# A pooling kernel: where the stores and the small first load are issued

## The chip, the cores and the metric

The kernel runs on one core of a Trainium2 chip. The metric is device time in microseconds, the median of several executions. One execution of each kernel was also recorded by the hardware profiler; its views are what is read here.

## What is computed

The input is 32 x 256 x 4096 values in fp32 (134.22 MB). The output takes every four neighbours along the last axis and gives the square root of the mean of their squares (p = 2), 32 x 256 x 1024 values (33.55 MB):

```python
for i in range(out_length):
    window = np.abs(x[:, :, 4*i:4*i+4]) ** p
    result[:, :, i] = (np.mean(window, axis=-1)) ** (1.0 / p)
```

Windows never cross a row, so the kernel treats the input as one flat array.

## The kernel before

The flat array is cut into 20 **loads**, L0 to L19, of 128 partitions x 13184 values each (6.75 MB; the last one is 10808 wide), and one **odd piece** of 840 x 128 values (0.43 MB), laid out as 30 partitions x 3584. Three input tiles (`xt`) take the loads in turn, so L3 goes into the tile of L0, and so on. Two output tiles (`ot`, 128 x 6592) take the results. Two loads make one **group** and share an output tile; the last two loads are groups of their own whose results go into a free input tile.

Each load goes through these steps:

- **SP** issues the DMA that brings the load (line 82). It waits until VectorE (DVE) has summed the load that held the tile before.
- **ScalarE (ACT)** squares the tile in place (line 168).
- **DVE** sums every four squares into the output tile: one reduce for the first 15 loads (line 111), two adds for the later ones (lines 122 and 124). One part of load 18 is squared on DVE (line 165).
- When a group is summed, **ACT** takes the roots in place (line 102, the function `root`). A group's root is put on ACT's queue one load later (two for group 8), behind the next load's square.
- A **store** (line 99, the function `store`) takes the group out. Groups 0 to 6 are stored from ACT's queue; groups 7 to 10 (`late`) from SP's queue, behind all loads.

The odd piece is loaded first (line 132) into part of an output tile, squared and summed on DVE (lines 137 and 139), rooted on ACT (line 143) and stored from ACT's queue (line 144). Its root and store stand at the head of ACT's queue, before L0's square.

The order on each engine is the order in which the program calls its instructions: the scheduling is manual, and each engine works through its queue in order. A DMA issue is an instruction of the queue that it is on: it waits there for its data, and what stands behind it waits too. Transfers of SP's queue and of ACT's queue run on the same DMA engines.

In the kernel before, `root` does not store: it puts the group into the list `held`, and the main loop empties the list after it has put the next square and its sum on their queues:

```python
            total_sum(ots[g][:, summed:summed + step // k], v, i)

            while held:
                store(held.pop(), nc.scalar)
            while pending and pending[0][0] <= done - LAGS.get(pending[0][1], 1):
                root(*pending.pop(0)[1:])
```

Of the kernel before, what the change touches and what calls it, by code (L numbers as in the profile page):

```python
# [9 lines left out]
def kernel(  # L10
# [15 lines left out]
    nc = tc.nc  # L26
# [5 lines left out]
    P = nc.NUM_PARTITIONS  # L32
    fp32 = mybir.dt.float32
    Act = mybir.ActivationFunctionType
    xf = x.rearrange("b c l -> (b c l)")
    of = out.rearrange("b c l -> (b c l)")
    total = xf.shape[0] // P
# [5 lines left out]
    ODD = 840  # L43
# [26 lines left out]
    def block(flat, g, div):  # L70
        at, width = sum(columns[:g]) * P // div, columns[g] * P // div
        return flat[at:at + width].rearrange("(p w) -> p w", p=P)
# [4 lines left out]
    def load(i):  # L77
        s, at, w, _ = loads[i]
        v = x_tiles[s % X_SLOTS][:, at:at + w]
        g = group_of[i]  # L80
        src = sum(loads[j][2] for j in range(firsts[g], i))
        nc.sync.dma_start(out=v, in_=block(xf, g, 1)[:, src:src + w])  # L82
        xs[i] = v
# [10 lines left out]
    def follows(ins, before):  # L94
        for b in before:
            tc.declare_no_dep(ins.ins, b.ins, reason="follows from other waits")

    def store(g, queue):
        stores[g] = queue.dma_start(out=block(of, g, k), in_=ots[g])

    def root(g, o, ends):
        r = nc.scalar.activation(out=o, in_=o, func=Act.Sqrt, scale=1.0 / k)  # L102
        follows(r, by_act[:-1] + list(stores.values()))
        by_act.append(r)
        if ends and g not in late:
            held.append(g)

    def total_sum(o, v, i):
        add = mybir.AluOpType.add
        if i < PAIRS:  # L110
            r = nc.vector.tensor_reduce(  # L111
                out=o, in_=v.rearrange("p (n j) -> p n j", j=k),
                axis=mybir.AxisListType.X, op=add,
            )
            follows(r, sums[:-1])
            sums.append(r)
            return

        q = v.rearrange("p (n j) -> p n j", j=k)
        front = v[:, 0:v.shape[1] // 2]  # L120
        h = front.rearrange("p (n j) -> p n j", j=2)
        r = nc.vector.tensor_tensor(out=h, in0=q[:, :, 0:2], in1=q[:, :, 2:4], op=add)  # L122
        follows(r, sums[:-1] + by_load)
        r = nc.vector.tensor_tensor(out=o, in0=h[:, :, 0], in1=h[:, :, 1], op=add)  # L124
        follows(r, sums[:-1])
        sums.append(r)


    Q = 30
    odd = ODD * P // Q  # L130
    t = o_tiles[1][0:Q, 0:odd]
    nc.sync.dma_start(out=t, in_=xf[(total - ODD) * P:total * P].rearrange("(p w) -> p w", p=Q))  # L132
    ahead = 0
    while ahead < n and loads[ahead][0] < X_SLOTS:
        load(ahead)
# [4 lines left out]
        out=o, in_=t.rearrange("p (n j) -> p n j", j=k),  # L140
# [4 lines left out]
        out=of[(total - ODD) * P // k:total * P // k].rearrange("(p w) -> p w", p=Q), in_=o,  # L145
    )
    pending = []
    held = []
    done = 0
    for i in range(n):  # L150
        s, _, w, chunks = loads[i]
        while ahead < n and loads[ahead][0] < s + X_SLOTS:
            load(ahead)
            ahead += 1
        g = group_of[i]
        if i == firsts[g]:
            t, first = (o_tiles[g % O_SLOTS], 0) if g not in in_x else (x_tiles[in_x[g][0]], in_x[g][1])
            ots[g] = t[:, first:first + columns[g] // k]
            summed = rooted = 0
        assert sum(chunks) == w  # L160
        c = 0
        for step in chunks:
            v = xs[i][:, c:c + step]
            if (i, c) in ON_DVE:
                r = nc.vector.tensor_tensor(out=v, in0=v, in1=v, op=mybir.AluOpType.mult)  # L165
                follows(r, sums[:-1])
            else:
                r = nc.scalar.activation(out=v, in_=v, func=Act.Square)  # L168
                follows(r, by_act[:-1])
                by_act.append(r)  # L170
            total_sum(ots[g][:, summed:summed + step // k], v, i)

            while held:
                store(held.pop(), nc.scalar)
            while pending and pending[0][0] <= done - LAGS.get(pending[0][1], 1):
                root(*pending.pop(0)[1:])
            done += 1
            c += step
            summed += step // k
            ends = summed == columns[g] // k  # L180
            if ends or i in FINE or (i in ENDS and c == w):
                pending.append((done - 1, g, ots[g][:, rooted:summed], ends))
                rooted = summed
    for job in pending:
        root(*job[1:])
# [37 lines left out]
```

## Time and profile before

| | |
|---|---|
| Median of 3 runs | 394.55 us (393.78 to 394.77) |
| Profiled execution | 393.78 us |
| Its span | 392.0 us |
| DVE busy | 274.5 us (70%) |
| ACT busy | 275.3 us (70%) |
| Moved by DMA | 167.77 MB, 428 GB/s over the span |
| A load on SP's queue, issue to landing | 31.6 us (median of 19) |
| A store on ACT's queue, issue to landing | 27.2 us (median of 7) |
| The odd load, the odd store | 3.9 us, 7.1 us |
| One square, one reduce, one root (full size) | 11.19 us, 13.89 us, 5.68 us |

The span is the time from the first to the last event of the profiled execution; its own time is 1.78 us longer. In the profile's rows, `L168` is line 168 of the kernel; `xt<-in_x_dram` is a load, `out_dram<-ot` a store; `SPq` and `ACTq` are DMA issues on SP's and ACT's queues. What stands in brackets at the end of a timeline row is the idle time of the engine before it, and what ended that. The windows view gives, for a stretch of time, the busy time and count of instructions on DVE, ACT and GpSimd, then a clock that does not matter here (no TensorE work), the DMA share (the packets' own time, counted at their end, as a share of 16 engines' time: over short stretches it jumps above 1) and the rate in GB/s.

### The profile page before, as it was taken

What the parts mean: (1) busy time and instruction counts of PE and PEld (TensorE: products, weight loads), DVE (VectorE), ACT (ScalarE), POOL (GpSimd) and SP (SyncE); (2) the same over time, 40 slices, a digit from 0 to 9 for tenths busy, and PEclk for the clock granted to TensorE, in tenths of its full rate; (3) what the DMA queues carried; (4) which work ended last, traced back from release to release, by engine and by line L of the source; (5) the groups of instructions that cost most, each with busy time, mean ns of one, the idle gap of its engine ahead of it and who ended that gap; (6) DMA issues with size and microseconds to landing.
All of it is one profiled execution on the core that took longest, in us unless ns stands there. A gap on an engine that the chain in (4) does not pass through costs nothing.

```text
span 392.0 us, 183 instructions
## 1 busy us (share of the span) xinstructions
DVE 274.5 (70%) x36; ACT 275.3 (70%) x38; POOL 0.2 (0%) x4
## 2 busy tenths in 40 slices
DVE  5207898885769476948693869386939690989991
ACT  1095879909890999099909990998099809987991
POOL 0000000000000000000000000000000000000000
DMA  9899999899999999999899999999989998999997
GB/s 367 379 444 452 452 447 441 347 444 468 447 401 431 471 431 393 431 474 431 387 431 474 431 457 441 393 431 468 436 387 431 474 431 387 447 452 401 446 439 330
DMA packets 4554, 167.77 MB, mean 428 GB/s; under 512 B 526, under 2 KB 526, under 8 KB 556
## 3 DMA queue, kind: packets, MB, share of 16 engines
q1 hardware_dynamic: 3501, 144.04, 85.3%
q10 hardware_dynamic: 1053, 23.73, 14.1%
HBM read 134.22 MB, written 33.55 MB: 428 GB/s over the span
## 4 chain that ended last, share of the span: by engine, by line
DMA 56%; DVE 22%; ACT 19%; SPq 0%; issue 0%
DMA xt<-in_x_dram 56%; ACT xt L168 19%; DVE ot L111 18%; DVE xt L122 3%; DVE ot L124 1%; DVE xt L124 1%; ACT xt L102 1%; SPq L132 0%; SPq L82 0%
## 5 line engine op out<-in xcount | busy, mean ns | idle before, releaser
L168 ACT ACTIVATE xt<-xt 128x13184 f32<-128x13184 f32 (+4 forms) x23 | 217.4, 9458 | 97.0 <-DMA xt<-in_x_dram 97.0
L111 DVE TENSOR_REDUCE ot<-xt 128x3296 f32<-128x13184 f32 x15 | 208.3, 13885 | 88.0 <-ACT xt L168 88.0
L102 ACT ACTIVATE ot<-ot 128x6592 f32<-128x6592 f32 x9 | 51.1, 5680 | 0.0
L122 DVE TENSOR_TENSOR xt<-xt 128x3296 f32<-128x3296 f32 (+5 forms) x9 | 34.5, 3835 | 16.5 <-ACT xt L168 16.4
L124 DVE TENSOR_TENSOR ot<-xt 128x3296 f32<-128x3296 f32 (+1 forms) x4 | 10.9, 2733 | 0.1
L143 ACT ACTIVATE ot<-ot 30x896 f32<-30x896 f32 x1 | 0.9, 948 | 10.5 <-DVE ot L139 10.5
L124 DVE TENSOR_TENSOR xt<-xt 128x1448 f32<-128x1448 f32 (+4 forms) x5 | 7.0, 1409 | 0.2
L137 DVE TENSOR_TENSOR ot<-ot 30x3584 f32<-30x3584 f32 x1 | 3.9, 3878 | 4.7 <-DMA ot<-in_x_dram 4.7
L102 ACT ACTIVATE xt<-xt 128x3296 f32<-128x3296 f32 (+3 forms) x4 | 5.8, 1445 | 1.1 <-DVE xt L124 1.1
L165 DVE TENSOR_TENSOR xt<-xt 128x5792 f32<-128x5792 f32 x1 | 6.2, 6182 | 0.0
L139 DVE TENSOR_REDUCE ot<-ot 30x896 f32<-30x3584 f32 x1 | 3.9, 3874 | 0.0
L143 ACT ACT_TABLE_LOAD x1 | 1.3, 1283 | 0.7 <-PEq L204 0.7
L204 POOL MEMSET const-bfloat16-1.0<- 128x1 bf16 x1 | 0.1, 103 | 0.0
L204 POOL MEMSET const-uint8-127<- 128x1 uint8 x1 | 0.1, 103 | 0.0
L204 POOL MEMSET const-float32-1.0<- 128x1 f32 x1 | 0.1, 100 | 0.0
L204 POOL MEMSET const-float32-0.0<- 128x1 f32 x1 | 0.1, 99 | 0.2 <-issue 0.2
## 6 DMA issues: line engine op xcount, KB each, us to landing
xt<-in_x_dram SPq DMA_DIRECT2D x19, 6592.0 KB, 31.6
out_dram<-ot ACTq DMA_DIRECT2D x7, 3296.0 KB, 27.2
out_dram<-ot SPq DMA_DIRECT2D x2, 3296.0 KB, 23.9
xt<-in_x_dram SPq DMA_DIRECT2D x1, 5404.0 KB, 23.9
out_dram<-xt SPq DMA_DIRECT2D x1, 1648.0 KB, 11.0
out_dram<-xt SPq DMA_DIRECT2D x1, 1351.0 KB, 6.6
ot<-in_x_dram SPq DMA_DIRECT2D x1, 420.0 KB, 3.9
out_dram<-ot ACTq DMA_DIRECT2D x1, 105.0 KB, 7.1
```

Of the source, the lines that this page charges most:

```text
L102: r = nc.scalar.activation(out=o, in_=o, func=Act.Sqrt, scale=1.0 / k)
L111: r = nc.vector.tensor_reduce(out=o, in_=v.rearrange("p (n j) -> p n j", j=k), axis=mybir.AxisListType.X, op=add,)
L122: r = nc.vector.tensor_tensor(out=h, in0=q[:, :, 0:2], in1=q[:, :, 2:4], op=add)
L124: r = nc.vector.tensor_tensor(out=o, in0=h[:, :, 0], in1=h[:, :, 1], op=add)
L137: nc.vector.tensor_tensor(out=t, in0=t, in1=t, op=mybir.AluOpType.mult)
L139: nc.vector.tensor_reduce(out=o, in_=t.rearrange("p (n j) -> p n j", j=k), axis=mybir.AxisListType.X, op=mybir.AluOpType.add,)
L143: nc.scalar.activation(out=o, in_=o, func=Act.Sqrt, scale=1.0 / k)
L165: r = nc.vector.tensor_tensor(out=v, in0=v, in1=v, op=mybir.AluOpType.mult)
L168: r = nc.scalar.activation(out=v, in_=v, func=Act.Square)
L204: nc = _bacc.Bacc("TRN2", target_bir_lowering=False, num_devices=1)
```

## The change

Two things are moved, and no arithmetic is changed. The stores of groups 0 to 6 are issued on ACT's queue directly behind the group's root, and the list `held` is gone. The load of the odd piece is issued from ACT's queue, where it is the first instruction, ahead of the load of ACT's function table; SP's queue begins with L0.

```diff
@@ root @@
         if ends and g not in late:
-            held.append(g)
+            store(g, nc.scalar)
...
     t = o_tiles[1][0:Q, 0:odd]
-    nc.sync.dma_start(out=t, in_=xf[(total - ODD) * P:total * P].rearrange("(p w) -> p w", p=Q))
+    nc.scalar.dma_start(out=t, in_=xf[(total - ODD) * P:total * P].rearrange("(p w) -> p w", p=Q))
...
     pending = []
-    held = []
     done = 0
...
             total_sum(ots[g][:, summed:summed + step // k], v, i)
-
-            while held:
-                store(held.pop(), nc.scalar)
             while pending and pending[0][0] <= done - LAGS.get(pending[0][1], 1):
                 root(*pending.pop(0)[1:])
```

## The prediction

> **What bounds the kernel now.** I began with the page's line for the DMA engines and its queue table, because the kernel does little arithmetic for each byte:
>
> ```profile
> DMA  9899999899999999999899999999989998999997
> q1 hardware_dynamic: 3501, 144.04, 85.3%
> q10 hardware_dynamic: 1053, 23.73, 14.1%
> HBM read 134.22 MB, written 33.55 MB: 428 GB/s over the span
> ```
>
> The two queues (q1 is SP, q10 is ScalarE: their megabytes are the sizes of the transfers issued there) fill 99.4% of 16 engines' span. DVE and ACT are busy 70% each. Next, the windows view, whose last two columns are DMA share and GB/s:
>
> ```profile
> 2.00:50.00 48.00, 24.47 (x4) 23.34 (x4) 0.00 (x0) 1.00 1.01 429
> 50.00:340.00 290.00, 208.37 (x17) 212.43 (x23) 0.00 (x0) 1.00 1.00 434
> 340.00:390.00 50.00, 41.62 (x17) 38.22 (x11) 0.00 (x0) 1.00 0.99 425
> ```
>
> The engines are full from the first bytes to the last, at one rate, whether loads run alone (2 to 50) or with stores between them. So only three things can move the end: when the first bytes flow, whether the engines ever run dry, and the rate. At 434 GB/s the 167.77 MB need 386.6 us of the 392.0.
>
> The chain of waits says otherwise at first sight: 56% DMA, 22% DVE, 19% ACT. But it follows three buffers round a ring: load, square, sum, next load. While one buffer is squared and summed, the loads of the others fill the engines. I therefore measure a cover: at the moment SP issues a load, how long the load ahead of it still has to run. L8 (loads numbered from L0) goes out when the sum of L5 ends, 117.76 + 13.88 = 131.64, and L7 lands at 145.47: cover 13.8 us. L9 goes out at 153.09 and L8 lands at 166.90: 13.8 again. The thinnest is L3: out at 31.58 + 13.88 = 45.46, L2 landing at 51.52, 6.1 us. In data rather than landings I take off 2.9 us: the odd piece's about 2.3 from its last row (before 2.5) to its 4.62 landing (a first DVE start of 4.67 less 0.05), and about 0.6 from issue to first bytes (0.73 to no later than 1.3). That leaves 10.9 and 3.2 us.
>
> **Part 1, the stores.** Seven DMA issues (groups 0 to 6) move on ACT's queue from behind the next square to ahead of it. Nothing is added. Two periods of the timeline:
>
> ```profile
> 127.98 11.19 ACT L168 ACTIVATE xt<-xt 128x13184 f32<-128x13184 f32 x1 [10.25 <-DMA xt<-in_x_dram]
> 139.08 5.68 ACT L102 ACTIVATE ot<-ot 128x6592 f32<-128x6592 f32 x1
> 145.47 11.19 ACT L168 ACTIVATE xt<-xt 128x13184 f32<-128x13184 f32 x1 [0.71 <-DMA xt<-in_x_dram]
> 145.48 0.34 ACTq L99 DMA_DIRECT2D out_dram<-ot  x1
> ```
>
> The issue follows the square's start within 0.01 us, so the store waited only for the square to be released by its load. After the change the issue must wait for the root itself: 139.08 + 5.68 = 144.76, plus 0.03 (the gap between the odd root's end, 12.49 + 0.95, and its issue at 13.47), so about 144.79. It leaves 0.7 us sooner. Five stores (groups 2 to 6) gain that; group 1 gains 1.0 us (root ends 105.54, issue was 106.61); group 0 gains nothing (root ends 68.30, issue was 68.33).
>
> Queued behind the issue is the next square, and who waits for that is the sum on DVE, then SP's load. The price is 0.03 + 0.34 + some 0.05 to start = 0.42 us per store. For groups 1 to 6 it lies in ACT's wait for the load (0.69 to 1.00 us). For group 0 it is exposed: L3's square, which began at 68.20 overlapping the root's end, begins near 68.7; its sum ends 0.5 us later and L6 goes out at 93.8, with L5 landing at 106.54. Nothing runs dry, and ACT then idles 9.4 us before L4 anyway. Cost to the end: 0. Uncovered, it would be 7 x 0.42 = 2.9 us.
>
> An earlier store can also take one of its rows in ahead of a load row: one 26.4 KB row costs 0.98 us on its engine at 434/16 = 27.1 GB/s, so L8, L10 and the others that share with a store may land up to 1 us later. The next root then ends up to 1 us later too (184.65 against L9's landing at 184.37), and that square starts about 0.7 us late. ACT idles 10 us before each following load, so it does not add up. L9's own landing does not move, since the bytes ahead of it are the same. Store landings come no later, so the sums that reuse an output tile are not held: store 0 lands at 68.33 + 28.5 = 96.8 and the sum that overwrites its tile starts at 99.98.
>
> **Part 2, the small first load.** It leaves SP (0.45 us, L132) for ACT, where it stands ahead of the table load. SP's L0 goes out at 0.73 instead of 1.24; L1, L2 follow. The table load (1.28 us) starts about 0.6 us later, under the wait for the odd sum.
>
> Does L0 gain 0.51 us? The first microseconds by the windows view:
>
> ```profile
> 1.00:2.00 1.00, 0.00 (x0) 1.00 (x1) 0.00 (x0) 1.00 0.73 215
> 2.00:3.00 1.00, 0.00 (x0) 0.01 (x1) 0.00 (x0) 1.00 1.02 268
> 3.00:4.00 1.00, 0.00 (x0) 0.00 (x0) 0.00 (x0) 1.00 2.17 791
> ```
>
> By 4.00 us, 215 + 268 + 791 = 1,274 KB had moved, which is 2.94 us at 434 GB/s: the engines have in effect been full since 1.06. They were moving the odd piece while L0 was issued. The same bytes must still pass, and the first issue stays at 0.73. The gain therefore lies between 0 and 1.06 - 0.73 = 0.33 us, and I take 0.1. A loss at the start is possible only if the second queue delays the first; the first issue on ACT took 0.64 us (L144), so the odd rows come at most some 0.2 us later, beside rows of L0 that fill the engines.
>
> [...]
>
> What it costs: the odd piece loses its place. Its two rows per engine now interleave with L0's. The nearest row is the odd store, also 30 rows, issued beside loads:
>
> ```profile
> 17.00:18.00 1.00, 0.00 (x0) 0.00 (x0) 0.00 (x0) 1.00 2.08 898
> 18.00:19.00 1.00, 0.00 (x0) 0.00 (x0) 0.00 (x0) 1.00 0.00 0
> 19.00:20.00 1.00, 0.00 (x0) 0.00 (x0) 0.00 (x0) 1.00 2.10 898
> ```
>
> and its line among the DMA issues (last number: us to landing):
>
> ```profile
> out_dram<-ot ACTq DMA_DIRECT2D x1, 105.0 KB, 7.1
> ```
>
> 898 instead of the usual 844 GB/s is 54 KB more: 15 of its rows beside each set of load rows, two sets, landing after 7.1 us. So the odd load lands at 0.73 + 7.1 + 2 x 0.4 (larger rows) = 8.6, at most 10.5 if two load rows go first (1.3 to first bytes, three load rows of 1.95 at that rate, two odd rows of 0.53, 2.3 to land). Then 7.8 us on DVE, 1.0 root, 0.64 store: ACT is free between 18.1 and 20.0. L0's square starts at 20.36. It is hidden, with 0.4 to 2.3 us left, and behind that stands L3's cover of 3.2 us. Cost 0.
>
> [...] The rows above show a switch after every load row.
>
> **Sum.** 393.78 is the profiled execution (span 392.0 plus 1.78 around it). Minus 0.1 at the start, plus 0 for stores and odd piece: 393.68. The median of the three runs lies 0.77 above the profiled one, so 394.45, say **394.4**.
>
> **The rivals.**
> *The odd piece is served late (slower, 0.10).* If its rows wait for all of L0, it lands near 20.3. ACT is in order: 20.3 + 7.8 + 1.0 + 0.7 = 29.8 for L0's square instead of 20.36. Its sum ends at 54.9, L3 goes out at 55 instead of 45.46, and the engines, out of data at 49.2, stand dry until 55.5: 6.3 us, 400.9. It decides once the odd load lands after about 14 us (10.9 that ACT covers plus 3.2). Against it: the alternating rows.
> *ACT's issues become exposed (slower, 0.12).* One to seven stores at 0.42 us: 394.9 to 397.5. It needs covers of 10.9 us in the steady part to be less than I think. The tail is tighter: the last store goes out at 384.6 and its 1.38 MB are the last 3.2 us before 390.1, so its bytes are due at 386.9, 1.7 us after they could first flow; a slip beyond that shows in full.
> *The start gains more (faster, 0.15).* Saving 0.51 us of issue and all of the odd piece's 0.99 us (0.43 MB) gives 1.5 us, 393.0. The full engines speak against it.
> *It changes nothing* is part of my forecast.
>
> **How the numbers follow.** A measurement of this kernel can tell about 0.3%, 1.2 us, from no change. My forecast has 0.58, inside that. Slower by more: 0.10, 0.12, and 0.05 for a rate that suffers from the shifted overlap, in all 0.27. Faster 0.15. The range runs from the fast rival's 393.0 to 397.0: it takes in the start's bounds and nearly all of the exposed issues, and leaves out the late odd piece and the rest.
>
> **What would show it.** Right: the store issues at the root's end, some 0.7 us ahead of the square; L0 issued at 0.73, odd landing at 8 to 10.5; the square of L0 near 20.3; DMA share 1.00 from 2 to 340; last load landing at 368 and the chain still DMA-led. Wrong: L0's square well after 20.4, a DMA share under 0.97 between 45 and 60, squares late by more than 1 us in every period, or a steady rate away from 434 GB/s.

## The result and the profile after

The changed kernel is slower: 395.91 us in the median of six runs (395.55 to 396.20) against 394.22 for the kernel before (now six runs too), ratio 1.0042 with a 95% interval of 1.0029 to 1.0055, so 1.7 us. The profiled execution took 395.82 us, its span 394.0 instead of 392.0.

The page's lines for the DMA engines and the queues of the changed kernel:

```profile
DMA  9999999999999999999999999999999999999997
q1 hardware_dynamic: 3456, 143.61, 84.9%
q10 hardware_dynamic: 1098, 24.16, 14.3%
HBM read 134.22 MB, written 33.55 MB: 426 GB/s over the span
```

The engines are still busy 99.2% of the span, with the same bytes. Nothing runs dry; something is slower while it runs. The windows view says where (last column GB/s):

```profile
2.00:50.00 48.00, 22.26 (x4) 24.03 (x4) 0.00 (x0) 1.00 0.98 403
50.00:340.00 290.00, 208.61 (x17) 211.18 (x23) 0.00 (x0) 1.00 1.00 434
340.00:390.00 50.00, 43.60 (x17) 39.57 (x12) 0.00 (x0) 1.00 0.99 427
```

The long middle has its 434 GB/s as before. Only the first stretch lost: 403 instead of 429. Narrowed down to the first ten microseconds of transfers, the kernel before:

```profile
1.00:11.00 10.00, 6.30 (x2) 1.01 (x1) 0.00 (x0) 1.00 0.98 381
```

and the changed kernel:

```profile
1.00:11.00 10.00, 0.00 (x0) 1.28 (x1) 0.00 (x0) 1.00 0.96 301
```

80 GB/s less over 10 us is 800 KB, or 1.84 us at 434 GB/s (the view counts a row whole where it starts, so this is rough; row by row it comes to 1.69 us, below). Nearly the whole loss of the span is there, before the first square and 60 us before the first group's store. The landings agree. The changed kernel's timeline, first the odd piece and L0, then one period in the middle, then the last load:

```profile
0.74 0.65 ACTq L132 DMA_DIRECT2D ot<-in_x_dram  x1
12.57 3.88 DVE L137 TENSOR_TENSOR ot<-ot 30x3584 f32<-30x3584 f32 x1 [12.57 <-DMA ot<-in_x_dram]
21.37 0.35 ACTq L144 DMA_DIRECT2D out_dram<-ot  x1
22.31 11.19 ACT L167 ACTIVATE xt<-xt 128x13184 f32<-128x13184 f32 x1 [0.97 <-DMA xt<-in_x_dram]
...
130.65 11.19 ACT L167 ACTIVATE xt<-xt 128x13184 f32<-128x13184 f32 x1 [11.22 <-DMA xt<-in_x_dram]
141.75 5.68 ACT L102 ACTIVATE ot<-ot 128x6592 f32<-128x6592 f32 x1
147.46 0.34 ACTq L99 DMA_DIRECT2D out_dram<-ot  x1
147.84 11.19 ACT L167 ACTIVATE xt<-xt 128x13184 f32<-128x13184 f32 x1 [0.42 <-ACT ot L102]
...
370.46 5.70 ACT L167 ACTIVATE xt<-xt 128x6592 f32<-128x6592 f32 x1 [0.84 <-DMA xt<-in_x_dram]
```

and in the kernel before the odd piece, the squares of L0 and of the last load:

```profile
4.67 3.88 DVE L137 TENSOR_TENSOR ot<-ot 30x3584 f32<-30x3584 f32 x1 [4.67 <-DMA ot<-in_x_dram]
...
20.36 11.19 ACT L168 ACTIVATE xt<-xt 128x13184 f32<-128x13184 f32 x1 [6.92 <-DMA xt<-in_x_dram]
...
368.44 5.70 ACT L168 ACTIVATE xt<-xt 128x6592 f32<-128x6592 f32 x1 [0.85 <-DMA xt<-in_x_dram]
```

The odd piece landed at 12.5 us (11.8 after its issue, where it had taken 3.9), L0 at 22.3 instead of 20.3. In the period shown of the changed kernel, the store leaves 0.03 us after the root's end (147.43) and the next square waits 0.42 us for it, as the prediction had it. But that 0.42 us is not what the end lost: the last load's square starts at 370.46 instead of 368.44, the same 2.0 us late as L0's.

**Reading single rows.** A transfer is cut into rows, one for each partition (the 19 full loads are 2,432 rows of 52.7 KB, 128 each; the odd piece is 30 rows of 14.3 KB); the packed trace has the start and length of each, but not the engine, and the views do not list them. A full load row of 52.7 KB takes 1.95 us in the steady part. I call *loss* what all rows that start in a stretch took beyond their bytes at that rate, divided by 16 engines. In the changed kernel the first rows of L0 took 2.3 to 3.6 us, and most of the second and third, beside the odd rows, 2.4 to 3.0. From the fourth on they took 1.95. The rows also correct a line of mine ahead of the prediction: the windows view counts a row where it starts, not where it ends.

### The profile page after: what moved, and what is told of

It reads as the page before. It is cut to its first block, busy times and chain, and to the rows that moved or that the text cites. A ratio compares the mean times of both kernels' runs of the same rounds, so it can differ in the third digit from the quotient of the medians.

```text
span 394.0 us, 182 instructions
## 1 busy us (share of the span) xinstructions
DVE 274.5 (70%) x36; ACT 275.4 (70%) x38; POOL 0.2 (0%) x4
## 3 DMA queue, kind: packets, MB, share of 16 engines
q10 hardware_dynamic: 1098, 24.16, 14.3%
## 4 chain that ended last, share of the span: by engine, by line
DMA 50%; ACT 28%; DVE 19%; another core or an unknown queue 1%; issue 0%; ACTq 0%; SPq 0%
DMA xt<-in_x_dram 50%; ACT xt L167 25%; DVE ot L111 14%; DVE xt L122 3%; ACT ot L102 3%; DVE ot L124 1%; DVE xt L124 1%; ACT xt L102 1%; ACTq L99 0%; SPq L82 0%
## 6 DMA issues: line engine op xcount, KB each, us to landing
ot<-in_x_dram ACTq DMA_DIRECT2D x1, 420.0 KB, 11.8
```

## The experiments

Theory S: the loss is made at the start, by the second part of the change. Its rival, theory I: ACT's issues, the first part. Below S stood three causes: P, the odd piece's 30 partitions make the engines meet in few places; Q, each change between two queues costs time; C, long rows are slow when they come first. A fourth, K, was added after the first four runs: long rows at the very start put the engines out of step, and short rows ahead of them keep them in step. All experiments but the second keep the stores of the kernel before. The last column has the ends of the last sixteen rows of L19, taken as one for each engine: the earliest, the median, the latest; the distance from the median to the latest is called *lag*. The numbers of all runs:

| kernel | ratio to before (95%) | loss per engine: 0 to 14 us | 14 to 45 | 60 to 85 | L19's last rows end: first, middle, last engine |
|---|---|---|---|---|---|
| before | | 0.98 | 0.03 | 0.41 | 367.40, 367.55, 367.96 |
| changed | 1.0042 (1.0029 to 1.0055) | 2.67 | 0.02 | 0.02 | 368.44, 368.98, 370.04 |
| odd_act_only | 1.0054 (1.0042 to 1.0066) | 2.75 | 0.02 | 0.02 | 368.45, 369.07, 370.05 |
| stores_only | 1.0000 (0.9989 to 1.0010) | 1.22 | 0.02 | 0.14 | 367.76, 367.96, 368.44 |
| odd_act_128 | 1.0038 (1.0026 to 1.0050) | 0.71 | 0.07 | 1.01 | 367.76, 368.00, 369.49 |
| odd_act_128_late | 1.0027 (1.0018 to 1.0037) | 0.69 | 0.03 | 0.77 | 367.40, 367.53, 369.12 |
| odd_act_split | 1.0024 (1.0015 to 1.0032) | 2.36 | 0.03 | 0.02 | 367.91, 368.91, 369.20 |
| odd_second | 1.0032 (1.0020 to 1.0045) | 0.86 | 1.68 | 0.02 | 368.24, 368.72, 369.84 |
| odd_second_64 | 1.0040 (1.0026 to 1.0053) | 0.74 | 1.64 | 0.02 | 368.28, 368.68, 369.34 |
| odd_second_128 | 1.0024 (1.0013 to 1.0035) | 0.79 | 0.07 | 0.87 | 367.52, 367.72, 369.12 |
| odd_sp_64 | 1.0002 (0.9991 to 1.0012) | 1.19 | 0.04 | 0.06 | 367.68, 367.85, 368.19 |
| odd_sp_120 | 1.0011 (1.0001 to 1.0021) | 1.06 | 0.03 | 0.65 | 367.64, 367.88, 368.87 |
| odd_sp_128 | 1.0011 (1.0001 to 1.0021) | 0.64 | 0.10 | 0.67 | 367.29, 367.48, 369.40 |

The losses are from one profiled execution each. The kernel before and stores_only do the same up to the first store, and they differ by 0.24 us at the start and by 0.27 at the store: differences of that size between two lines of the table say little.

**1. The second part alone** (odd_act_only).

```diff
-    nc.sync.dma_start(out=t, in_=xf[(total - ODD) * P:total * P]...)
+    nc.scalar.dma_start(out=t, in_=xf[(total - ODD) * P:total * P]...)
```

> Only the odd piece's load moves to ACT's queue; the stores stay behind the next square. Theory S (the start): the whole loss is made in the first 15 us, where L0's rows and the odd piece's rows alternate; so this kernel is as slow as the changed one, 1.5 to 2.0 us over before, odd landing near 12.5 and L0 near 22.3. Theory I (ACT's issues exposed): no difference from before, because no store has moved.

396.39 us against 394.24: 2.15 us slower, the odd piece landing at 12.8 and L0 at 22.6:

```profile
12.87 3.88 DVE L137 TENSOR_TENSOR ot<-ot 30x3584 f32<-30x3584 f32 x1 [12.87 <-DMA ot<-in_x_dram]
...
22.62 11.19 ACT L168 ACTIVATE xt<-xt 128x13184 f32<-128x13184 f32 x1 [0.98 <-DMA xt<-in_x_dram]
```

The whole change's loss is here. With the next run, theory I falls.

**2. The first part alone** (stores_only).

```diff
-            held.append(g)
+            store(g, nc.scalar)
...
-            while held:
-                store(held.pop(), nc.scalar)
```

> Only the stores move to directly behind the root; the odd piece is loaded first on SP as before. Theory S: within 0.3 us of before; L0 lands at 20.3, the store issues at the root's end and every second square starts up to 0.5 us late with nothing lost at the end. Theory I: 1.5 to 2.9 us over before, built up store by store, with the last load landing near 370.

393.95 us against 394.24: no difference, within 0.1%. In its timeline the square waits 0.42 to 0.45 us for the store's issue after groups 0, 2, 4 and 6, covered each time by ACT's idle time before the next load (8.6 to 9.9 us, 9.49 here). After groups 1, 3 and 5 it still waits for its load. The square behind group 2's store begins at 146.24 instead of 145.47, and the one after it at 166.91, where it was 166.90:

```profile
145.85 0.34 ACTq L99 DMA_DIRECT2D out_dram<-ot  x1
146.24 11.19 ACT L167 ACTIVATE xt<-xt 128x13184 f32<-128x13184 f32 x1 [0.42 <-ACT ot L102]
166.91 11.19 ACT L167 ACTIVATE xt<-xt 128x13184 f32<-128x13184 f32 x1 [9.49 <-DMA xt<-in_x_dram]
```

**3. Another shape for the odd piece, from ACT** (odd_act_128): the same bytes in 128 partitions x 840.

```diff
-    Q = 30
+    Q = 128
-    nc.sync.dma_start(out=t, ...)
+    nc.scalar.dma_start(out=t, ...)
```

> Odd piece from ACT's queue (stores as before), laid out as 128 partitions x 840 instead of 30 x 3584: the same bytes in 8 short rows per engine, each engine's rows in its own partitions. Theory P (the 30 rows of the odd piece lie in 30 partitions, so that engines that write elsewhere meet there and hold each other up): most of the loss goes, within 0.5 us of before or faster by up to 1 us. Theory Q (every change between the two queues costs about 0.9 us of an engine's time): up to eight changes instead of two, so slower than the changed kernel, L0 landing later than 22.3. Theory C (the first large rows of a run are slow by themselves when they come first): L0's first rows still take 2.5 us and more, 0.5 to 1.5 us over before.

The extra loss at the start is gone: 0.71 us per engine, less than in the kernel before. The rows show some eight turns of an odd row of 0.13 us and then a load row of 1.95 on each engine: a change of queue costs nothing here, and Q falls. C forecast the time (0.5 to 1.5 us over before; 1.4 measured) and the slow first rows (most of L0's first rows take 2.5 us and more), and P, with 0.5 at most, missed it. But C does not explain the changed kernel's loss at the start: L0's rows come first here too, and the stretch as a whole is no worse than before. By the table and the timeline, other things took the time. The odd piece now alternates with all eight rows of L0, lands at 20.7, and holds L0's square until 23.7:

```profile
23.34 0.34 ACTq L144 DMA_DIRECT2D out_dram<-ot  x1
23.73 11.19 ACT L168 ACTIVATE xt<-xt 128x13184 f32<-128x13184 f32 x1 [0.42 <-ACT ot L143]
36.42 11.19 ACT L168 ACTIVATE xt<-xt 128x13184 f32<-128x13184 f32 x1 [1.51 <-DMA xt<-in_x_dram]
48.86 0.33 SPq L82 DMA_DIRECT2D xt<-in_x_dram  x1
52.05 11.19 ACT L168 ACTIVATE xt<-xt 128x13184 f32<-128x13184 f32 x1 [4.44 <-DMA xt<-in_x_dram]
```

L3 then goes out at 48.9 with L2 landing at 52.0, and its first rows, from 50.4 on, took up to 2.7 us. The last engine is 1.5 us behind the middle one at L19, and the first store lost 1.01 us instead of 0.41. How much of the 1.4 us each made was not separated.

**4. The same with the root later** (odd_act_128_late): the odd root and store behind L0's square.

```diff
             total_sum(ots[g][:, summed:summed + step // k], v, i)
+            if i == 0:
+                nc.scalar.activation(out=odd_out, in_=odd_out, func=Act.Sqrt, scale=1.0 / k)
+                stores["odd"] = nc.scalar.dma_start(...)
```

> Odd piece from ACT's queue in 128 x 840, with its root and store behind L0's square, so that the square does not wait for the late odd piece; stores as before. In the run with 128 partitions ahead of the square, L3 went out at 48.8 and its first rows took up to 2.7 instead of 1.95 us. If that thin cover of L3 made the loss there: now L3 goes out near 45.9, those rows take 1.95, and the time is 0.3 to 0.8 us over before (what the start out of step costs, theory K). If the cover had no part in it: again 1.4 us over before.

The start now runs at 421 GB/s, from the same queue and with the same bytes as the changed kernel's 301:

```profile
1.00:11.00 10.00, 0.00 (x0) 1.28 (x1) 0.00 (x0) 1.00 1.04 421
```

L3 goes out at 45.9 and its rows lose nothing. The time is 1.0 us over before, a little above what was expected. The middle engine ends L19 at 367.53, level with the kernel before; the last one is 1.6 us behind it.

**5. The odd piece second, on one queue** (odd_second): it follows L0 on SP; root and store as in 4.

```diff
-    nc.sync.dma_start(out=t, ...)
...
         load(ahead)
         ahead += 1
+        if ahead == 1:
+            nc.sync.dma_start(out=t, ...)
```

> Odd piece from SP's queue behind L0, instead of ahead of it; its root and store stand behind L0's square on ACT (one more table load of 1.28 us there, before L1 lands); stores as before. One queue only, and L0's large rows come first. Theory C: L0's first rows take 2.5 us or more, and the loads land late by about 1 us as against before, time +0.5 to +1.5 us. Theory P: L0's first rows take about 1.95 us, and the odd rows hold up the rows of L0's end or L1's start as they did before at the start, so no more than 0.3 us from before, or faster. Theory Q: no change of queue in the first 20 us, so no loss, within 0.3 us of before.

Slower by 1.3 us (395.58), with 1.68 us lost per engine where the odd rows lie between the last rows of L0 and the first of L1 (up to 3.5 us for one). So neither ACT's queue nor the start is needed for it: the 30 rows of the odd piece do it here as well, beside long rows. The forecasts fared badly: P and Q had at most 0.3 us over before. C had the time (0.5 to 1.5) and the slow first rows of L0 (2.4 to 3.4 us), but those lost 0.86 us per engine, as in the runs with 128 partitions; the larger part came later, where C puts nothing.

**6. and 7. The same with 64 and with 128 partitions** (odd_second_64, odd_second_128).

```diff
-    Q = 30
+    Q = 64    # and 128
```

> The odd piece behind L0 on SP's queue, 64 partitions x 1680 (16 engines, four rows each) instead of 30 x 3584; root behind L0's square, stores as before. With 30 partitions the rows around the odd piece lost 1.7 us per engine. [...] If the number of partitions or the row length alone counts: the loss there falls to 0.3 to 1.0 us, L1 near 36.7 to 37.3, time 0.2 to 0.9 us over before.

> The same with 128 partitions x 840. [...] If a second transfer between two long ones costs by itself: 1.0 to 1.6 us over before, as with 30 partitions.

The square of L1 in odd_second:

```profile
38.01 11.19 ACT L166 ACTIVATE xt<-xt 128x13184 f32<-128x13184 f32 x1 [3.86 <-DMA xt<-in_x_dram]
```

in odd_second_64:

```profile
37.59 11.19 ACT L166 ACTIVATE xt<-xt 128x13184 f32<-128x13184 f32 x1 [4.30 <-DMA xt<-in_x_dram]
```

and in odd_second_128:

```profile
36.00 11.19 ACT L166 ACTIVATE xt<-xt 128x13184 f32<-128x13184 f32 x1 [3.73 <-DMA xt<-in_x_dram]
```

With 64 partitions the loss is the same, 1.64 us (time 395.54, 1.3 over before); with 128 it is 0.07, and L1 lands 2.0 us sooner than with 30 (the time stays 0.7 us over before; lag and first store are larger in the table). Twice the partitions and half the row length changed nothing, so a cost that shrinks steadily with either does not fit; one reading that does is which partitions they are, the first 64 or all. But it does not fit odd_sp_120 (below): its 120 partitions reach well past the first 64, yet it lost 1.06 us at the start, like 30 and 64 partitions there (0.98 to 1.22) and unlike 128 (0.64). P as experiment 3 had it, with each engine's odd rows in its own partitions, is not excluded, but no trace shows which partitions an engine writes. Why 128 is cheaper stays open.

**8. Short rows of L0 first** (odd_act_split): as 1, with L0 in two transfers.

```diff
-        nc.sync.dma_start(out=v, in_=block(xf, g, 1)[:, src:src + w])
+        cuts = [0, 840, w] if i == 0 else [0, w]
+        for lo, hi in zip(cuts, cuts[1:]):
+            nc.sync.dma_start(out=v[:, lo:hi], in_=block(xf, g, 1)[:, src + lo:src + hi])
```

> Odd piece (30 x 3584) from ACT's queue, stores as before, but L0 comes on SP in two transfers: 840 columns first (rows of 3.4 KB), then the other 12344. Theory K: short rows start the run, the engines stay in step within 0.5 us, and the loss falls from 2.1 to 0.5 to 1.3 us. Theory P alone: the loss comes from the odd rows beside L0's rows and stays at 1.7 to 2.3 us.

395.21, 1.0 us over before, within what K expected (0.5 to 1.3), and not what P alone expected (1.7 to 2.3): the last engine ends L19 0.3 us behind the middle one instead of 1.0. Yet the loss of the rows at the start stays at 2.36 (2.75 in experiment 1), so the odd rows cost nearly as much as there.

**9. to 11. Other shapes, first on SP** (odd_sp_128, odd_sp_64, odd_sp_120); nothing else differs from the kernel before.

```diff
-    Q = 30
+    Q = 128    # and 64, and 120
```

> The kernel before with one size changed: the odd piece, first on SP as before, is 128 partitions x 840 instead of 30 x 3584. Theory P (meeting in few partitions): its rows then take 1.06 us per engine instead of the 1.9 us they took before (1.8 to 3.7), L0 lands at 19.4 to 19.6, and the time is 0.6 to 0.9 us under before. Theory K (long rows at the very start put the engines out of step; short rows ahead of them keep them in step) alone: the engines stay in step as before and the time is within 0.3 us of before.

> As before, odd piece first on SP, 64 partitions x 1680: 16 engines, four rows each, half the partitions. [...] Theory P in the form that only the number of partitions counts, or a theory that the long rows of the odd piece are slow for their length: about 1.1 to 1.5 us, and a gain of 0.4 to 0.8 us, near that of 128 partitions.

> The kernel before with the odd piece first on SP as 120 partitions x 896: spread over nearly all partitions, but on 15 engines as in the kernel before. In 128 partitions it saved 0.3 us per engine at the start and then lost more because one engine fell 1.9 us behind the middle one. If a sixteenth engine that carries an odd part is what falls behind: the engines stay within 0.6 us and the time is 0.2 to 0.5 us under before. If one falls behind whenever the odd piece does not hold all engines up first: again 0.2 to 1.0 us over before.

odd_sp_64 is the kernel before again (394.11 against 394.25; 1.19 us lost at the start), without the gain of 0.4 to 0.8 us that the number of partitions or the length of the rows should have brought. odd_sp_128 lost less at the start (0.64 instead of 0.98), the way P said, but the time was 394.85 against 394.25 where P had 0.6 to 0.9 us under before: the last engine was 1.9 us behind the middle one in the profile, and 0.67 us went at the first store. K falls with it as I had put it, for here short rows came first. odd_sp_120, where by its expectation one engine carries no odd row (in the kernel before the odd rows ran 15 at a time, twice), ends with a lag of 1.0 us and the same ratio (394.65 against 394.28): leaving an engine out does not settle it. It also lost at the start like the narrower layouts (1.06 us, where 30 and 64 partitions lost 0.98 and 1.19), and no run shows why.

**What stays open.** Two smaller terms move between these kernels. One is an engine that ends 0.3 to 1.9 us behind the middle one. In most runs it falls behind in its first rows (by up to 1.6 us), in odd_sp_120 later (0.2 us after the first rows, 1.0 at the end); since all engines have nearly the same bytes left (in the rows of the kernels before and after, each of 16 chains has 152 of the 2,432 full rows, eight for each full load), it stays behind. The other is a loss of up to 1.0 us on the load rows between 70 and 75 us, as the first rows of the first store begin; it was 0.41 in the kernel before, 0.02 in the changed one, and larger where the start was quicker. I found no rule for either that all runs obey, and no version beat the kernel before. For the time P missed in four runs (odd_act_128, odd_second, odd_act_split, odd_sp_128); what bears it out is the loss of the rows and the landings. Spreading the odd piece over 128 partitions removed its loss and did not bring the time back.

## Why the prediction was wrong

The forecast of 394.4 with 0.58 for no measurable change was wrong; 395.91 lies in the range of 393.0 to 397.0, but by luck: its upper part stood for exposed stores, and the stores cost nothing.

- **Stores: right.** Cost 0, by the 0.42 us per store that ACT's wait covers. After groups 0, 2, 4 and 6 the next square began 0.42 to 0.44 us behind the root's end; after groups 1, 3 and 5 it waited 0.69 to 0.72 us, for its load as before. stores_only measures 1.0000, so the mechanism held as well as the number.
- **The step that failed: the odd piece's cost.** I wrote "It is hidden, with 0.4 to 2.3 us left" and "Cost 0". That priced only who waits for the odd piece: DVE, the root, ACT, L3's cover. It took the transfer itself as "the same bytes must still pass". They do not pass at the same price: beside long rows the odd rows cost the engines about 1.7 us more (2.67 against 0.98 at the start). In the kernel before the odd rows started at 1.74 to 2.73 us, all ahead of L0's first at 2.83. My model row, the odd store, had the wrong direction and only a quarter of the bytes, and I added 0.4 us per row for the size.
- **The landing.** 8.6 to at most 10.5 was predicted, 12.5 measured; L0's square near 20.3, measured 22.31. The mechanism that should have decided (rows alternate) was right, the length of the rows beside each other (mostly 2.4 to 3.0 us, not 1.95) was not.
- **"In effect full since 1.06".** This rested on rows counted at their end. They are counted where they start; the first rows begin at 1.74 in both kernels, and the kernel before had itself lost 0.98 us per engine by 14 us. The start's gain was not 0 to 0.33 but below nothing. The 2.9 us that the prediction takes off each cover come from the same reading: the last odd row ended at 3.80, 0.8 us before the landing at 4.62, and the first row began 1.0 us after its issue, which makes 1.8. Nothing hung on that.
- **The rivals.** The odd piece did not come behind all of L0; the issues did not become exposed; no gain at the start. What happened was the case I gave 0.05, "a rate that suffers from the shifted overlap": it suffered at the start.
- **The sum of the loss.** In the profiles the middle engine ends L19 1.43 us later: 1.69 at the start, less 0.39 at the first store, 0.13 elsewhere. The last engine lies 1.06 behind it instead of 0.41, 0.65 more. Together 2.08, for a span 2.0 longer.
- **The second issuing queue.** No gain showed from it: L0 was issued at 0.73 instead of 1.24, and its square began at 22.31 instead of 20.36. The odd rows came between single rows of L0: 15 started at 4.25 to 5.52 us, behind first rows of L0, and 15 at 7.73 to 9.01, behind second ones.

## What to carry to other kernels

Where the DMA engines are full (99.2 to 99.4% of the span here), a moved transfer is not free because "the bytes are the same": ask how it is laid out over the partitions and what will run beside it. Laid out over 30 or 64 partitions, a piece of 0.43 MB cost the engines 1.6 to 1.7 us beside full-height loads, whether it came from SP's queue (30 and 64) or from ACT's (30, as the rise over the kernel before); over all 128 it cost under 0.1. And most of an early loss stays in a stream that never runs dry: of 1.69 us lost at the start, the middle engine was still 1.43 late at the end. Check the time as well as the loss: with 128 partitions off the head of the queue the kernel was still 0.7 to 1.4 us over before.

## What the runs showed of the hardware

- A change between two queues, row by row, cost nothing measurable: odd rows of 0.13 us and load rows of 1.95 us alternated some eight times on each engine in odd_act_128.
- 30 and 64 partitions behaved alike (1.68 and 1.64 us lost beside long rows); 128 lost 0.07. First in the run, 120 partitions lost 1.06 us, like 30 and 64 (0.98 to 1.22); 128 lost 0.64.
- The first long rows of the changed kernel took 2.3 to 3.6 us instead of 1.95; where L0 came first, the engines came out of such rows up to 1.6 us apart (4.28 to 5.86 in odd_act_only).
- In odd_act_128 a load issued only 3.2 us before the one ahead of it landed had first rows of up to 2.7 us; issued 6.3 us ahead, in odd_act_128_late, they took 1.95.
